# New places in on-chip memory for the operands of an encoder's matmuls

## The chip, the cores and the metric

The kernel runs on one core of a Trainium2 chip. The metric is device time in microseconds (us) of one execution; less is better. The core has five engines: TensorE (PE) multiplies matrices, VectorE (DVE), ScalarE (ACT) and GpSimd (POOL) work element by element, and SyncE (SP) issues most DMA transfers. The on-chip memory holds tiles of 128 partitions; a tile has the same byte place in every partition, and this case is about that place. A matmul on TensorE has two operands in that memory: the stationary one (128 columns), which a weight load (PEld in the profile) brings into the array, and the moving one (here 256 or 512 columns), which streams through it. The sum goes to PSUM, a separate memory.

## The reference

Two encoder layers over 512 tokens of width 1024, 16 heads of 64, all in float32. Cut to what matters:

```python
for layer in range(2):
    h = rms_norm(x, norm_mix_pre[layer])
    h = neighbourhood_attention(h, ...) if layer == 0 else dilated_attention(h, ...)
    x = x + rms_norm(h, norm_mix_post[layer])
    h = rms_norm(x, norm_ffn_pre[layer])
    h = (silu(h @ w_gate[layer]) * (h @ w_up[layer])) @ w_down[layer]     # d_ff = 2816
    x = x + rms_norm(h, norm_ffn_post[layer])
```

Layer 0 attends over an 8 x 64 grid in windows with a learned bias; layer 1 over three dilations (1, 4, 16), which are merged by their softmax denominators. Each mixer begins with products for q, k and v and ends with an output product.

## The kernel before, in words

**Products.** Every float32 operand of a large product is split into a rounded high part and a low remainder, both in the type fp32r (`split`, L365 on ACT and L366 on DVE). One product is then three matmuls (`mm3`, L377 to L379): high by high, high by low, low by high. Blocks of 2 x 2 are multiplied with seven products instead of eight (`Seven`, `Values`, `down`); the sums of operands that this needs are made on POOL and DVE, or by DMA.

**Stages in order of time.** Values of layer 0 (tiles `vp_n`), its q and k units (`pp_n`) with the window attention between them, the output product (`yo`), gate and up products (`gu`, from 258 us to 495 us), the down product (`yd`, to 597 us); then layer 1: values (`vp_d`, `vd`, to 739 us), q and k units (`pp_d`, to 1073 us) with the dilated attention between them, and again `yo`, `gu` (1143 us to 1373 us) and `yd` (to 1477 us). In all stages but two the moving operand has 256 columns; in `yo` and `yd` it has 512.

**Who lies where.** `rxa` and `rxc` hold the transposed activations that are operands; `rxb` holds three more pairs of them for the mixers. The weights, split, lie in eight slots (`h_...`, `l_...` from `wslot`), and one of the seven weight operands alternates between `vmem` and an end of `rxc` (`w22_ring`). `mem` holds hidden activations and what attention needs. `wm`, `memc`, `ao`, `akl` are tiles that follow each other in the same place at the end of memory. In `gu`, `pp_n` and `pp_d` weights are stationary and activations move; in `vp`, `vd`, `yo` and `yd` activations are stationary and weights move. For `yd` the split activations lie in a ring of five places in `rxc`, and the split weights in the eight slots.

**Places.** The tile pools lay tiles out one after the other. Before, the start of each, in bytes modulo 512, is

| tile | before | changed |
|---|---|---|
| `rxa`, `rxc`, `mem` | 160 | 128 |
| `vmem` | 160 | 448 |
| `rxc` from element 80 (`rxs`, new) | | 448 |
| raw weights, slots `h_...` and `l_...` | 480 | 448 |
| `rxb` | 480 | 128 |
| `wm` | 480 | 128 |
| `ao`, `akl`, `memc` | 480 | 480 |

160 and 480 are 32 more than a multiple of 64; 128 and 448 are multiples of 64. Operands are cut from the tiles at multiples of 256 bytes or more.

**Order.** The order of the work on each engine is written by a planner inside the kernel (`Order`): it takes the recorded instructions with their dependences, estimates each one's time (`_cost`), runs eight passes over them, and pins the best order on every engine. It knows sizes and types and nothing of places. Each wait on a chip is a semaphore that another engine raises.

## Time and profile before

| | |
|---|---|
| median of 3 runs | 1484.54 us (1484.52 to 1489.98) |
| the profiled execution | 1487.69 us; its span, first to last instruction, 1485.9 us |
| granted TensorE clock, mean | 0.996 of full speed |
| PE busy | 1442.8 us, 97% of the span, 10788 matmuls |
| PE weight loads | 1333.1 us, 90% |
| DVE, ACT, POOL busy | 1196.8 us (81%), 904.1 us (61%), 542.4 us (37%) |
| moved by DMA | 253.22 MB, 170 GB/s |

A row of groups gives a line of the kernel, the engine, the operation, the tiles (written <- read; for a matmul the moving operand stands first), the shape, the count, busy time and the mean duration of one. The duration of a matmul is that of its passage through the array; matmuls overlap each other, and what a matmul costs in a dense stream is the distance from its start to the start of the next. This document calls that distance the pace. It is read from the timeline, where each row begins with the start in us and the duration.

### The profile page before, as it was taken

The page shows a single profiled execution, that of the slowest core. Times are in us where ns is not written, and L with a number is a line of the kernel's source. Part 1 is how long each engine was busy: PE and PEld are TensorE (multiplying, and loading weights), DVE is VectorE, ACT ScalarE, POOL GpSimd, SP SyncE. Part 2 cuts the span into 40 slices and gives each one's busy share as a digit, 9 for nine tenths or more (in the row PEclk, how much of TensorE's full clock was granted, in tenths as well). Part 3 has the DMA queues.
Part 4 walks back from the last instruction along what each step waited for, and adds up shares of the span by engine and source line. Part 5 has one row for each costly group of instructions (what it writes and reads, how often), then busy time and mean ns, then how long its engine had stood idle before and what let it go on. Part 6 is the DMA issues. An engine that isn't in the chain of part 4 may idle for free.

```text
span 1485.9 us, 27934 instructions
## 1 busy us (share of the span) xinstructions
PE 1442.8 (97%) x10788; PEld 1333.1 (90%) x10788; DVE 1196.8 (81%) x1876; ACT 904.1 (61%) x1819; POOL 542.4 (37%) x398
## 2 busy tenths in 40 slices
PE   7999999899999999999999999999999999999997
PEld 6988877899999888899999999989977999999886
DVE  5499967699889788797689788787657989998877
ACT  4478874555555567544467778876675654555664
POOL 5345425544231001665555444334204644330001
PEclk9999999899999999999999999999999999999999
DMA  5346487677333664435433343333766788834662
GB/s 200 139 177 179 155 286 206 227 221 212 114 112 114 204 220 162 168 126 187 142 100 101 93 145 116 100 133 103 237 206 214 200 243 243 252 126 149 203 208 92
DMA packets 86645, 253.22 MB, mean 170 GB/s; under 512 B 19312, under 2 KB 31600, under 8 KB 84464
## 3 DMA queue, kind: packets, MB, share of 16 engines
q1 hardware_dynamic: 77696, 197.69, 40.4%
q0 software_dynamic: 8672, 53.48, 13.9%
q8 instruction: 85, 1.39, 0.4%
q14 instruction: 48, 0.39, 0.1%
q10 hardware_dynamic: 144, 0.26, 0.0%
HBM read 229.24 MB, written 68.29 MB: 200 GB/s over the span
## 4 chain that ended last, share of the span: by engine, by line
PE 77%; DVE 8%; ACT 7%; DMA 3%; issue 3%; POOL 1%; SPq 0%; POOLq 0%; DVEq 0%; ACTq 0%
PE gu L377 10%; PE gu L378 9%; PE gu L379 9%; PE pp_d L377 5%; PE pp_d L379 4%; PE pp_d L378 4%; PE yd_s L377 3%; PE yd_s L379 3%; PE yd_s L378 3%; PE yd_pp L377 2%; PE yd_pp L379 2%; PE yd_pp L378 2%; PE sb L1274 2%; PE yo L377 2%; PE yo L379 1%
## 5 line engine op out<-in xcount | busy, mean ns | idle before, releaser
L585 POOL TENSOR_TENSOR rs_yd<-v_yd,mhalf 128x1 f32<-128x1 f32 x8 | 8.3, 1043 | 261.3 <-DVE v_yd L583 261.3
L378 PE MATMUL gu<-rxa,h_b 128*128 128x256 f32 x352 | 100.0, 284 | 2.5 <-DVE rxa L602 2.5
L377 PE MATMUL gu<-rxc,h_a 128*128 128x256 f32 x352 | 99.7, 285 | 2.0 <-ACT h_a L365 1.2
L377 PE MATMUL gu<-rxa,h_c 128*128 128x256 f32 x352 | 99.7, 283 | 1.3 <-DVE memc L839 1.1
L378 PE MATMUL gu<-rxc,h_a 128*128 128x256 f32 x352 | 99.7, 284 | 1.2 <-DVE rxc L602 1.0
L377 PE MATMUL gu<-rxa,h_b 128*128 128x256 f32 x352 | 99.7, 284 | 1.2 <-ACT rxa L601 1.2
L379 PE MATMUL gu<-rxa,l_b 128*128 128x256 f32 x352 | 99.6, 283 | 0.2 <-DVE l_b L366 0.2
L379 PE MATMUL gu<-rxc,l_a 128*128 128x256 f32 x352 | 99.1, 282 | 0.0
L378 PE MATMUL gu<-rxa,h_c 128*128 128x256 f32 x352 | 98.7, 280 | 0.0
L379 PE MATMUL gu<-rxa,l_c 128*128 128x256 f32 x352 | 98.3, 280 | 0.0
L365 ACT ACTIVATE rxc<-mem 128x512 fp32r<-128x512 f32 (+2 forms) x90 | 55.9, 624 | 65.9 <-PE yd_pp L378 33.8
L445 POOL TENSOR_TENSOR r_d<-r_d 128x512 f32<-128x512 f32 x24 | 36.1, 1506 | 161.0 <-DVE l_ad L366 122.9
L445 POOL TENSOR_TENSOR r_gu<-r_gu 128x512 f32<-128x512 f32 x20 | 30.6, 1529 | 149.8 <-DVE l_a L366 102.4
L366 DVE TENSOR_TENSOR rxc<-mem,rxc 128x512 fp32r<-128x512 f32 (+2 forms) x90 | 64.4, 719 | 19.5 <-ACT rxc L365 19.2
L445 POOL TENSOR_TENSOR raw<-raw 128x512 f32<-128x512 f32 x24 | 38.0, 1582 | 99.4 <-DVE l_a L366 74.7
L378 PEld LDWEIGHTS gu<-rxa,h_b 128*128 128x128 f32 x352 | 67.6, 192 | 2.7 <-DVE rxa L602 2.7
L377 PEld LDWEIGHTS gu<-rxc,h_a 128*128 128x128 f32 x352 | 67.1, 192 | 2.8 <-ACT h_a L365 1.4
L377 PEld LDWEIGHTS gu<-rxa,h_c 128*128 128x128 f32 x352 | 66.5, 189 | 2.9 <-DVE memc L839 1.3
L378 PEld LDWEIGHTS gu<-rxc,h_a 128*128 128x128 f32 x352 | 67.2, 191 | 1.8 <-DVE rxc L602 1.8
L377 PEld LDWEIGHTS gu<-rxa,h_b 128*128 128x128 f32 x352 | 67.3, 192 | 1.5 <-ACT rxa L601 1.4
L1238 ACT ACTIVATE mem<-mem 128x256 f32<-128x256 f32 x128 | 63.8, 504 | 7.5 <-DVE mem L1237 7.3
L379 PEld LDWEIGHTS gu<-rxa,l_b 128*128 128x128 f32 x352 | 67.4, 191 | 0.4 <-DVE l_b L366 0.4
(610 smaller groups left out, 6157.7 us busy)
## 6 DMA issues: line engine op xcount, KB each, us to landing
wsum<-wd POOLq DMA_DIRECT2D x24, 1408.0 KB, 12.1
r_d<-dil_qk SPq DMA_DIRECT2D x48, 512.0 KB, 4.1
raw<-wg SPq DMA_DIRECT2D x24, 512.0 KB, 5.1
raw<-wu SPq DMA_DIRECT2D x24, 512.0 KB, 8.4
wsum<-wsum POOLq DMA_DIRECT2D x8, 1408.0 KB, 10.3
raw<-wsum SPq DMA_DIRECT2D x22, 512.0 KB, 4.3
r_gu<-wg SPq DMA_DIRECT2D x20, 512.0 KB, 3.8
r_gu<-wu SPq DMA_DIRECT2D x20, 512.0 KB, 4.9
```

Of the source, the lines that this page charges most:

```text
L365: act.activation(h, src, AF.Copy)
L366: dve.tensor_sub(l, src, h.bitcast(F32))
L377: i = pe.matmul(o, s[0], m[0], start=start, stop=False, skip_group_check=True)
L378: pe.matmul(o, s[0], m[1], start=False, stop=False, skip_group_check=True)
L379: pe.matmul(o, s[1], m[0], start=False, stop=stop, skip_group_check=True)
L445: self.added = e[0].tensor_add(q[0], q[0], q[2])
L585: pool.tensor_tensor(r, v, mhalf, op=ALU.pow)
L1238: act.activation(pr[:, f], pr[:, f], AF.Exp, bias=st[:, c:c + 1], scale=-1.0, accum_out=st[:, c + 2:c + 3])
L1274: pe.matmul(ss[hd][:, f0:f0 + P], qf[rw, block(c)], kf[rw, block(c)], start=True, stop=True)
```

## The change

The tiles and parts of tiles move to the places in the right column above. By the roles of the operands: moving activations of the 256-wide products and stationary activations of `vp`, `vd` and `yo` come to 128, split weights to 448. In `yd`, stationary activations come to 448, where its moving weights are. In `yo`, most moving weights come to 128 (`wm`, `rxb`, parts of `rxa`), where its stationary activations are. Counted over the fp32r matmuls of the program, by the distance of the two operands' starts modulo 512:

| moving operand | distance | before | changed |
|---|---|---|---|
| 256 wide | 192 or 320 bytes | 6232 | 7880 |
| 256 wide | same place | 1760 | 48 |
| 256 wide | other | 64 | 128 |
| 512 wide | 192 bytes | 1244 | 112 |
| 512 wide | same place | 64 | 1196 |

Besides, twenty one-column tiles of the norms become columns of one tile `few_small`, and the constant `mhalf` moves behind the weight slots. The tile `wm` gets 88 unused columns.

```diff
-MEM, ARENA = 14544, 9 * D
+MEM, ARENA = 14544, 9 * D + 88
+SHIFT = 80
...
+    zpool = ctx.enter_context(tc.tile_pool(name="zpool", bufs=1))
...
-    mhalf = cpool.tile([P, 1], F32, name="mhalf")
-    dve.memset(mhalf, -0.5)
...
     rxc = cpool.tile([P, 5 * D + 256], F32R, name="rxc")
+
+    mem = cpool.tile([P, MEM], F32, name="mem")
     vmem = cpool.tile([P, D], F32R, name="vmem")
 
-    mem = cpool.tile([P, MEM], F32, name="mem")
+    few_small = cpool.tile([P, 32], F32, name="few_small")
+    mhalf = zpool.tile([P, 48], F32, name="mhalf")[:, 0:1]
+    dve.memset(mhalf, -0.5)
+
+    rxs = rxc[:, SHIFT:SHIFT + 5 * D]
...
-    small_ = cycle(range(20))
+    small_ = cycle([few_small[:, i:i + 1] for i in range(20)])
...
-            return tagged(cpool, [P, n], F32, f"small_o{next(small_)}", name, 1)
+            return next(small_)
...
-        v_ = w22_ring(rxc[:, 4 * D:5 * D])
+        v_ = w22_ring(rxs[:, 4 * D:])
...
-        us = [None] * 2 + [hl(wm, 0, D), (wm[:, 2 * D:], vmem), hl(rxa, 8, D)] + [hl(rxb, 2 * i, D) for i in range(3)]
+        us = [None] * 2 + [hl(wm, 0, D), (wm[:, 2 * D:3 * D], vmem), hl(rxa, 8, D)] + [hl(rxb, 2 * i, D) for i in range(3)]
...
-        hl_ = ring(rxc, 0, D, 5)
+        hl_ = ring(rxs, 0, D, 5)
...
-    with arena("wm0", 3 * D, "right", F32R) as wm:
+    with arena("wm0", 3 * D + 88, "right", F32R) as wm:
...
-    q_, k_, kl_, ost_ = rxc[:, 0:D], rxc[:, D:2 * D], rxc[:, 2 * D:3 * D], ring(rxc, 3 * D, D, 1)
-    w22_ = w22_ring(rxc[:, 4 * D:5 * D])
+    q_, k_, kl_, ost_ = rxc[:, 0:D], rxs[:, D:2 * D], rxs[:, 2 * D:3 * D], ring(rxs, 3 * D, D, 1)
+    w22_ = w22_ring(rxs[:, 4 * D:])
...
-    vus, vslots = {}, cycle([hl(rxc, 0, D), hl(rxc, 2, D), (vmem, rxc[:, 4 * D:5 * D])])
+    vus, vslots = {}, cycle([hl(rxs, 0, D), hl(rxs, 2, D), (vmem, rxs[:, 4 * D:])])
```

The instructions stay the same in number and kind on every engine: 10390 matmuls before they are expanded for the chip, and as many after. Their order stays the same too, but for 46 matmuls, and a few rows of ACT and DVE beside them, at one place: PE at the end of `gu` of layer 0, where its last two units (numbers 20 and 21) meet the first products of `yd`. Before, PE has there:

```order
L379 MATMUL gu_21_5096<-rxa,l_b_21_5341 128x256
L377 MATMUL gu_21_5096<-rxa,h_b_21_5340 128x256
L378 MATMUL gu_21_5096<-rxa,h_b_21_5340 128x256
L379 MATMUL gu_21_5096<-rxa,l_b_21_5341 128x256
L377 MATMUL gu_20_4980<-rxa,h_c_20_5318 128x256
L378 MATMUL gu_20_4980<-rxa,h_c_20_5318 128x256
L379 MATMUL gu_20_4980<-rxa,l_c_20_5319 128x256
L377 MATMUL gu_20_4980<-rxa,h_c_20_5318 128x256
```

and in the changed kernel, at the same place:

```order
L385 MATMUL gu_21_5072<-rxa,l_b_21_5317 128x256
L383 MATMUL gu_21_5072<-rxa,h_b_21_5316 128x256
L383 MATMUL gu_20_4956<-rxa,h_c_20_5294 128x256
L384 MATMUL gu_20_4956<-rxa,h_c_20_5294 128x256
L385 MATMUL gu_20_4956<-rxa,l_c_20_5295 128x256
L383 MATMUL gu_20_4956<-rxa,h_c_20_5294 128x256
L384 MATMUL gu_20_4956<-rxa,h_c_20_5294 128x256
L385 MATMUL gu_20_4956<-rxa,l_c_20_5295 128x256
```

Two of the `gu_21` products with `rxa` moved some rows back, and those of `gu_20` came forward; the operands, the shapes and the number of rows are the same.

On POOL, the norms of the output product raise to the power -0.5 (L585 before, L591 now) between sums of weight operands. Before:

```order
L445 TENSOR_TENSOR r_gu_0_2881<-r_gu_0_2881 128x512
L585 TENSOR_TENSOR rs_yo_0_2594<-v_yo_0_2592,mhalf 128x1
L446 TENSOR_TENSOR r_gu_0_2881<-r_gu_0_2881 128x512
L873 DMA wsum_82<-wd 128x2x1408
L445 TENSOR_TENSOR r_gu_1_2916<-r_gu_1_2916 128x512
L585 TENSOR_TENSOR rs_yo_1_2607<-v_yo_1_2605,mhalf 128x1
```

and now:

```order
L451 TENSOR_TENSOR r_gu_0_2857<-r_gu_0_2857 128x512
L591 TENSOR_TENSOR few_small<-few_small,mhalf 128x1
L452 TENSOR_TENSOR r_gu_0_2857<-r_gu_0_2857 128x512
L879 DMA wsum_86<-wd 128x2x1408
L451 TENSOR_TENSOR r_gu_1_2892<-r_gu_1_2892 128x512
L591 TENSOR_TENSOR few_small<-few_small,mhalf 128x1
```

Nothing moved here; the small tiles have one name in place of many, and all engines together wait on semaphores at three instructions more than before, of some 4500.

More of the change, by code (lines that the diff above doesn't have):

```diff
@@ L1429, in encoder_kernel @@
     inner.close()
-    with arena("wm1", 3 * D, "right", F32R) as wm:
+    with arena("wm1", 3 * D + 88, "right", F32R) as wm:
         mix_out(1, a["dil_o"], rxb, wm, load_block)
```

## Prediction

> **What bounds the kernel now.** I read the page first: busy times, then the chain of work that ended last.
>
> ```profile
> span 1485.9 us, 27934 instructions
> PE 1442.8 (97%) x10788; PEld 1333.1 (90%) x10788; DVE 1196.8 (81%) x1876; ACT 904.1 (61%) x1819; POOL 542.4 (37%) x398
> PE 77%; DVE 8%; ACT 7%; DMA 3%; issue 3%; POOL 1%; SPq 0%; POOLq 0%; DVEq 0%; ACTq 0%
> ```
>
> TensorE is busy for 97% of the span and makes 77% of the chain. So time is gained or lost by what one matmul costs in a dense stream. That is the pace, from one start to the next, and the change touches nothing else on TensorE. I therefore looked in the timeline of PE for stretches without a wait and divided the distance of two rows by the matmuls between them. First, one piece of the values of layer 1, in which nothing waits:
>
> ```profile
> 700.01 0.28 PE L379 MATMUL vd<-rxc,rxb 128*128 128x256 f32 x1
> ...
> 711.91 0.28 PE L377 MATMUL vd<-h_cd,rxb 128*128 128x256 f32 x1
> 711.92 0.19 PEld L378 LDWEIGHTS vd<-l_cd,rxb 128*128 128x128 f32 x1
> 712.03 0.28 PE L378 MATMUL vd<-l_cd,rxb 128*128 128x256 f32 x1
> ...
> 714.79 0.28 PE L377 MATMUL vd<-rxc,rxa 128*128 128x256 f32 x1
> ```
>
> From 700.01 to 711.91 are 105 matmuls: 113.3 ns each. In them the two operands start 320 or 192 bytes apart modulo 512 (`rxc` and `vmem` at 160 against `rxb` at 480, the slots at 480 against `rxa` at 160). From 711.91 to 714.79 are 24: 120.0 ns each. There both lie at 480 (slot `h_cd` or `l_cd`, and `rxb`). The shape and the stage are the same; the places differ. The rows of 711.92 and 712.03 show what can meet: the weight load of the next matmul begins 0.01 us after the start of the present one, so that stationary and moving operand are read at the same time, from 480 both.
>
> Then a piece of `gu` of layer 0, and two of `yd`, of layer 0 and of layer 1:
>
> ```profile
> 443.21 0.28 PE L379 MATMUL gu<-rxa,vmem 128*128 128x256 f32 x1
> ...
> 453.69 0.28 PE L377 MATMUL gu<-rxc,h_a 128*128 128x256 f32 x1
> ...
> 500.04 0.39 PE L379 MATMUL yd_pp<-h_d0p,rxc 128*128 128x512 f32 x1
> ...
> 539.87 0.39 PE L379 MATMUL yd_s<-h_d0s,rxc 128*128 128x512 f32 x1
> ...
> 1380.05 0.40 PE L379 MATMUL yd_pp<-h_d1p,rxc 128*128 128x512 f32 x1
> ...
> 1419.94 0.40 PE L379 MATMUL yd_s<-h_d1s,rxc 128*128 128x512 f32 x1
> ```
>
> `gu`: 89 matmuls in 10.48 us, 117.8 ns, although all but the first of these operands are 320 bytes apart (weights at 480, activations at 160). `yd`: 174 in 39.83 us, 228.9 ns, and in layer 1 171 in 39.89 us, 233.3 ns, with the same operands at the same places. So place is not all: a stream finds one of two paces when it starts after a wait, and keeps it.
>
> The numbers have a common step. 120.0 less 113.3 is 6.7 ns, and 113.3 is 17 such steps, 120.0 is 18, 233.3 is 35. Sixteen steps for 256 columns would be 16 columns, or 64 bytes, a step. An operand of 1024 bytes that starts 32 bytes beyond a multiple of 64, as all of them do before, touches 17 pieces of 64 bytes and not 16. That fits a best pace of 17 steps, though it doesn't prove it: a fixed cost of one step fits as well.
>
> What could stop a faster TensorE? DVE, which makes the operands. The windows of both gate and up stages:
>
> ```profile
> core 0: us, PE busy (x) PEld busy (x) DVE busy (x) ACT busy (x) POOL busy (x), PEclk, DMA share, GB/s
> 258.00:488.00 230.00, 224.51 (x1860) 222.97 (x1861) 200.94 (x256) 123.41 (x211) 82.07 (x54) 0.98 0.54 170
> 1143.00:1366.00 223.00, 220.85 (x1858) 219.01 (x1857) 200.69 (x256) 121.88 (x211) 89.34 (x61) 1.00 0.72 211
> 495.00:587.00 92.00, 92.00 (x404) 75.50 (x403) 79.48 (x107) 62.34 (x94) 3.40 (x3) 1.00 0.61 196
> ```
>
> In `gu` DVE is busy for 401.6 of 453 us, 89%; in `yd` for 79.5 of 92.0, 86%, and PE without a break.
>
> **The change part by part.** It removes and adds no instruction on any engine; 46 matmuls of 10390 change rank at one place, which I cost at nothing, since they stand in the same `gu` stream with the same operands. One column of `few_small` in place of a small tile costs nothing either: three more waits in some 4600, at the norms of `yo`, whose work stands beside products. If that cover went, each would cost about one such operation on POOL, 1.04 us by the page, 3 us in all:
>
> ```profile
> L585 POOL TENSOR_TENSOR rs_yd<-v_yd,mhalf 128x1 f32<-128x1 f32 x8 | 8.3, 1043 | 261.3 <-DVE v_yd L583 261.3
> ```
>
> What is left is the pace. It has two causes: the distance of the operands, and the start at a multiple of 64. The second is in no row of before, since no large operand starts at one there. Bounds for a 256-wide matmul, then: above, 117.8 ns, the slower pace that a distance of 320 has now; nothing in the trace says that distance alone forbids it. Below, the weight load: each matmul needs one of 128 columns.
>
> ```profile
> 851.32 1.03 PE L1334 MATMUL t<-ident,mem 128*128 128x128 f32 x8
> L1334 PE MATMUL t<-ident,mem 128*128 128x128 f32 x256 | 36.6, 276 | 0.0
> ```
>
> Eight transposes of 128 columns, each with a weight load, take 1.03 us from the first start to the last end; less one duration of 0.276, over seven distances, that is 108 ns. So a 256-wide matmul lies between 108 and 117.8 ns. I take 112: between 108 and the 113.3 that the trace already has, nearer to the row. For a 512-wide matmul the same piece counting gives 33 steps with the present start and 32 without: 220 to 233.3 ns; I take 227, a little under the better pace of now, since what it loses beyond 33 steps is not explained.
>
> *Gate and up.* 22 units of 84 matmuls in each layer, 3696 in all. 528 of them lie at the same place now (`vmem` and the end of `rxc` against `rxa`), yet the piece from 443.21 shows 117.8 for the mixture, and some stretches run at 113.3; I take 117.6 as their mean. 117.6 less 112 is 5.6 ns, times 3696: 20.7 us. DVE would then be busy for 401.6 of 432 us, 93%, and what TensorE gains it waits for now and then: I let two thirds through, 14 us. Without DVE in the way it would be 20.7; if DVE lets nothing through, 0.
>
> *The other 256-wide products.* 8056 in the program less 3696 are 4360. Of these 1232 lie at the same place now (1760 less 528), at 120.0; the rest I put midway between 113.3 and 117.8, at 115.6. Mean 116.8; to 112 it is 4.8 ns, times 4360: 21 us. In these stages attention stands between the products, and the chain gives 23% to others than PE; again two thirds, 14 us.
>
> *The 512-wide products.* 1308, at 228.9 and 233.3 in about equal parts, 231 in the mean; to 227 it is 4 ns, 5 us. PE has no break there, so all of it counts.
>
> Sum: 14 + 14 + 5 = 33 us off a span of 1485.9, 1453 us. The profiled execution took 1487.69 us, 1.8 more than its span, and 3.2 more than the median of the runs, 1484.54. Off the median it makes 1451.5, so 1452 us.
>
> A rule speaks against all of this. The Trainium skill, SBUF — State Buffer, section Specifications (TRN2), gives lines of 16 bytes, by which a start at 32 beyond a multiple of 64 is as good as one at 0. The Trainium skill, TensorE: Matmul & The Clock Gate, section Step-by-step: what each phase is for, says that loading the next weights takes no read bandwidth from the running matmul, by which the distance of the operands should not matter. The trace disagrees with the second: 120.0 against 113.3 ns in neighbouring rows. On the first no row of before decides. By both the time would stay at 1484, which is the rival of no change below. The same page's section Back-to-back issue gap gives columns over 2.4 GHz plus 2.5 ns, an estimate of 109.2 ns for 256 columns; it would lie inside my bounds, and with it the two 256-wide terms would be some 31 and 33 us before what DVE holds back.
>
> **The rivals.**
>
> *All of the pace is gained.* The 256-wide matmuls come to 108 ns and the 512-wide ones to 220. Terms: 9.6 x 3696 = 35 us, 8.8 x 4360 = 38 us, 11 x 1308 = 14 us; with two thirds of the first two, 63 us: 1422. Half way to it from my case, 1437. For it: the exact 17 steps. Against: DVE at 200.7 of 223 us. Chance 0.22 that the time is under 1440.
>
> *DVE becomes the bound.* Pace falls as I say, but `gu` gains nothing, as DVE's two-operand work there waits for POOL and ACT as it does now; then 14 + 5 = 19 us: 1466, and with less elsewhere 1476. For it: 89% busy. Against: the waits of PE for DVE in the windows of `gu` are few now (224.5 and 220.9 us busy of 230 and 223). Chance 0.12.
>
> *No change: the start at 64 bytes does nothing.* What stays is the distance: 1712 matmuls fewer at the same place, at 120.0 less 117.8, 4 us, of which two thirds: 1482; if these came to 113.3, 11 us, two thirds of it 8: 1477. For it: `gu` at 117.8 with a distance of 320, and the two paces of `yd` at the same places. Chance 0.14.
>
> *Slower: the same place in the 512-wide products.* They go the other way: from 64 at the same place to 1196. In the 256-wide rows the same place costs one step of 6.7 ns; a moving operand twice as long could meet the weight load twice, 13.3 ns. 1132 more by 13.3 are 15 us, all on the path as PE has no break in `yd`; if the 64 bytes gain nothing and only the 4 us of distance come back, 1496. It decides from about 10 ns a matmul on, beyond what the other terms bring if they fail. Against it stand the few that lie at the same place now (`vmem` against `rxa` in `yo`; columns: shortest, median and longest duration) beside others of that line that don't:
>
> ```profile
> L378 PE MATMUL yo<-wm,rxa x16: 388/392/505, 218.2 to 1132.8; 128*128 128x512 f32 x16
> L378 PE MATMUL yo<-vmem,rxa x16: 388/393/401, 219.5 to 1134.2; 128*128 128x512 f32 x16
> ```
>
> 392 and 393 ns: no step between them. Chance 0.07.
>
> **How the numbers follow.** My case, 1440 to 1466, has 0.45; the full gain 0.22; DVE as the bound 0.12; no change 0.14; slower 0.07. A measurement of this kernel tells about 0.5% from no change, 7.4 us: faster is below 1477.1, slower above 1492. The first three cases and a little of the fourth's lower end make 0.80 for faster; the rest of the fourth 0.13 for the same; 0.07 for slower. The range goes from 1425, where the full gain with two thirds ends, to 1484, where no change begins to be a loss; what lies outside are the slower case and the ends of the others.
>
> **What would show it.** In the changed trace the neighbouring pieces of `vd` must have one pace, 113.3 or less, with no 120.0 left; this is the surest step. The pace of `gu` must be under 117.8 in long pieces; if there are rows under 113, the start at 64 bytes is what does it. `yd` must be at 229 or less in both layers; 240 would be the slower rival. In `gu`, PE's share of busy time must fall and waits on DVE rise by some 7 us. Wrong would be the prediction if `gu` keeps 117.8, or if paces fall and the span doesn't.

## The result: 0.75% faster, about a third of the forecast gain

The changed kernel takes 1477.45 us (median), the kernel before, on the same chip, 1489.98 us. The ratio is 0.9925, with a 95% interval of 0.9908 to 0.9943: 11 us faster by the ratio (12.5 by the medians), where 32 were forecast. The profiled execution of the changed kernel took 1475.85 us with a span of 1474.0, 11.9 us less than the span of before; this is the difference that the rest explains. On the page of the changed kernel the busy times and the chain now read:

```profile
span 1474.0 us, 27934 instructions
PE 1425.7 (97%) x10788; PEld 1317.0 (89%) x10788; DVE 1200.5 (81%) x1876; ACT 902.7 (61%) x1819; POOL 541.4 (37%) x398
PE 66%; DVE 15%; ACT 8%; DMA 4%; issue 4%; POOL 1%; SPq 0%; POOLq 0%; DVEq 0%; ACTq 0%
```

PE is busy for 17.1 us less and its weight loads (PEld) for 16.1; DVE, ACT and POOL stay within 4 us of before. PE's share of the chain falls from 77% to 66% and DVE's rises from 8% to 15%: part of what the products gained has turned into waits, as the table below shows.

The paces come from the timeline of PE, as in the prediction: first and last row of a stretch without a break, divided by the matmuls between them in the program. (`mm3` stands six lines lower in the changed kernel, at L383 to L385.) Values of layer 0, values of layer 1, gate and up of layer 1, and the down product of layer 1:

```profile
36.60 0.28 PE L383 MATMUL vp_n<-h_n,rxa 128*128 128x256 f32 x1
...
60.74 0.29 PE L383 MATMUL pp_n<-rxa,h_an 128*128 128x256 f32 x1
...
694.70 0.28 PE L384 MATMUL vd<-rxc,rxb 128*128 128x256 f32 x1
...
717.94 0.33 PE L383 MATMUL vd<-rxc,rxb 128*128 128x256 f32 x1
...
1262.75 0.28 PE L384 MATMUL gu<-rxa,h_c 128*128 128x256 f32 x1
...
1316.35 0.28 PE L385 MATMUL gu<-rxa,l_b 128*128 128x256 f32 x1
...
1364.62 0.39 PE L384 MATMUL yd_pp<-l_d1p,rxc 128*128 128x512 f32 x1
...
1451.88 0.39 PE L385 MATMUL yd_s<-h_d1x2b,rxc 128*128 128x512 f32 x1
```

`vp_n`: 205 matmuls at 117.8 ns, as before. `vd`: 205 at 113.4. `gu`: 473 in a row at 113.3 ns, where before the long stretches ran at 117.8. `yd` of layer 1: 385 at 226.7 ns, where it was 233.3. The 120.0 of before is in no stretch of the changed kernel. Nor is anything with 256 columns below 113.3.

The next table sets every start on PE of both profiled executions against the program. A distance from one start to the next of up to 124 ns (245 for 512 columns) counts as pace. Of a longer one, 116 ns (237) counts as pace and the rest as stall. "Net" is the difference of the two sums; pace in ns, the rest in us, before -> after.

```
stage           matmuls   pace             at that pace     stalls         net
gu, layer 0       1848    117.44 -> 113.97   217.0 -> 210.6   10.7 -> 12.0   -5.0
gu, layer 1       1848    117.40 -> 114.28   217.0 -> 211.2    5.3 ->  7.4   -3.7
vp_n               384    117.62 -> 117.62    45.2 ->  45.2    2.6 ->  2.6    0.0
pp_n               672    116.97 -> 115.72    78.6 ->  77.8    9.6 -> 11.6   +1.1
vp_d               192    117.68 -> 117.06    22.6 ->  22.5    4.4 ->  5.4   +0.8
vd                 840    116.02 -> 115.05    97.5 ->  96.6    4.5 ->  4.0   -1.3
pp_d              2016    116.62 -> 115.36   235.1 -> 232.6   16.2 -> 18.7    0.0
yo, both layers    384    230.9  -> 230.2     88.7 ->  88.4    4.1 ->  4.3    0.0
yd, layer 0        462    229.06 -> 226.89   105.8 -> 104.8    0.1 ->  0.1   -1.0
yd, layer 1        461    233.24 -> 226.76   107.5 -> 104.5    0.0 ->  0.0   -3.0
all others                                                                   +0.3
```

The rows add up to -11.8 us. At the pace alone they give 20.8 us, and the stalls grow by 8.6. Gate and up give 8.7 us net and the down product 4.0; everything else together loses 0.9. All of this is from one execution of each kernel.

The windows of the two `gu` stages (columns as in the prediction: length, then busy time of each engine) show how full DVE is there:

```profile
259.20:491.20 232.00, 225.24 (x1905) 222.15 (x1906) 206.39 (x263) 125.91 (x216) 83.68 (x54) 0.99 0.55 173
1137.60:1364.50 226.90, 223.88 (x1908) 220.39 (x1908) 207.37 (x264) 124.82 (x216) 88.98 (x61) 1.00 0.71 212
```

DVE is busy for 413.8 of 458.9 us, 90%; PE's idle time is 6.8 and 3.0 us. PE's waits for DVE in `gu`, added up, are 6.4 us, before 5.1; in the products of queries and keys, `pp_n` and `pp_d`, they are 7.5, before 4.2. Two rows that show the latter, in the view of PE's waits (total us, times, longest), of before:

```profile
PE pp_d L377 <- DVE pp_d L435: 1.2, 2, 0.8
...
PE pp_n L377 <- DVE mem L686: 0.5, 1, 0.5
```

and of the changed kernel:

```profile
PE pp_n L383 <- DVE mem L692: 2.0, 1, 2.0
...
PE pp_d L383 <- DVE pp_d L441: 1.6, 4, 0.9
```

### The profile page after: what moved, and what is told of

Read it like the earlier page. It is cut to its first block, busy times and chain, and to the rows that moved or that the text cites. A ratio compares the mean times of both kernels' runs of the same rounds, so it can differ in the third digit from the quotient of the medians.

```text
span 1474.0 us, 27934 instructions
## 1 busy us (share of the span) xinstructions
PE 1425.7 (97%) x10788; PEld 1317.0 (89%) x10788; DVE 1200.5 (81%) x1876; ACT 902.7 (61%) x1819; POOL 541.4 (37%) x398
## 4 chain that ended last, share of the span: by engine, by line
PE 66%; DVE 15%; ACT 8%; DMA 4%; issue 4%; POOL 1%; SPq 0%; POOLq 0%; DVEq 0%; ACTq 0%
PE gu L383 7%; PE gu L384 7%; PE gu L385 7%; PE pp_d L383 4%; PE pp_d L385 4%; PE pp_d L384 3%; PE yd_s L385 3%; PE yd_s L384 3%; PE yd_s L383 3%; PE yd_pp L384 2%; PE yd_pp L385 2%; PE yd_pp L383 2%; PE yo L383 2%; PE yo L385 1%; PE yo L384 1%
## 5 line engine op out<-in xcount | busy, mean ns | idle before, releaser
L591 POOL TENSOR_TENSOR rs_yd<-v_yd,mhalf 128x1 f32<-128x1 f32 x8 | 9.5, 1184 | 255.2 <-DVE v_yd L589 255.2
L383 PE MATMUL gu<-rxa,h_c 128*128 128x256 f32 x352 | 99.3, 282 | 3.1 <-DVE memc L845 1.4
L383 PE MATMUL gu<-rxc,h_a 128*128 128x256 f32 x352 | 97.7, 279 | 2.4 <-ACT h_a L371 1.5
L383 PE MATMUL gu<-rxa,h_b 128*128 128x256 f32 x352 | 98.6, 281 | 1.2 <-ACT rxa L607 1.2
L384 PE MATMUL gu<-rxc,h_a 128*128 128x256 f32 x352 | 98.0, 279 | 1.1 <-DVE rxc L608 1.0
L385 PE MATMUL gu<-rxa,l_b 128*128 128x256 f32 x352 | 98.6, 280 | 0.3 <-DVE l_b L372 0.3
L385 PE MATMUL gu<-rxc,l_a 128*128 128x256 f32 x352 | 97.3, 277 | 0.0
L385 PE MATMUL gu<-rxa,l_c 128*128 128x256 f32 x352 | 97.1, 277 | 0.0
L451 POOL TENSOR_TENSOR r_d<-r_d 128x512 f32<-128x512 f32 x24 | 33.4, 1391 | 162.2 <-DVE l_ad L372 123.5
L372 DVE TENSOR_TENSOR rxc<-mem,rxc 128x512 fp32r<-128x512 f32 (+2 forms) x90 | 64.3, 717 | 17.3 <-ACT rxc L371 17.1
L383 PEld LDWEIGHTS gu<-rxa,h_c 128*128 128x128 f32 x352 | 66.1, 188 | 5.9 <-DVE memc L847 2.0
L383 PEld LDWEIGHTS gu<-rxc,h_a 128*128 128x128 f32 x352 | 65.9, 188 | 3.4 <-ACT h_a L371 2.1
L383 PEld LDWEIGHTS gu<-rxa,h_b 128*128 128x128 f32 x352 | 67.0, 191 | 1.6 <-ACT rxa L607 1.4
L385 PEld LDWEIGHTS gu<-rxa,l_b 128*128 128x128 f32 x352 | 67.3, 191 | 0.5 <-DVE l_b L372 0.5
## 6 DMA issues: line engine op xcount, KB each, us to landing
wsum<-wd POOLq DMA_DIRECT2D x24, 1408.0 KB, 11.9
```

Source lines behind the costliest of these rows:

```text
L372: dve.tensor_sub(l, src, h.bitcast(F32))
L383: i = pe.matmul(o, s[0], m[0], start=start, stop=False, skip_group_check=True)
L384: pe.matmul(o, s[0], m[1], start=False, stop=False, skip_group_check=True)
L385: pe.matmul(o, s[1], m[0], start=False, stop=stop, skip_group_check=True)
L451: self.added = e[0].tensor_add(q[0], q[0], q[2])
L591: pool.tensor_tensor(r, v, mhalf, op=ALU.pow)
```

## The experiments

From here on, **distance** is the start of the moving operand less that of the stationary one, modulo 512 bytes. `gu` has its weights stationary (448 after the change) and its activations moving (128): a distance of 192, and it was 192 before as well, from 480 to 160. The value products `vp_n`, `vp_d` and `vd` have the activations stationary and the weights moving: 320. `yd` goes from 320 to 0.

**The start alone.** The kernel before, with every large operand 32 bytes nearer to the front: all start at a multiple of 64, and every distance is what it was.

```
-MEM, ARENA = 14544, 9 * D
+MEM, ARENA = 14544, 9 * D + 8
...
+    zpool = ctx.enter_context(tc.tile_pool(name="zpool", bufs=1))
...
-    mhalf = cpool.tile([P, 1], F32, name="mhalf")
-    dve.memset(mhalf, -0.5)
...
+    few_small = cpool.tile([P, 32], F32, name="few_small")
+    mhalf = zpool.tile([P, 128], F32, name="mhalf")[:, 0:1]
+    dve.memset(mhalf, -0.5)
...
```

> Only the start at a multiple of 64 bytes: all tiles move by 32 bytes, the distances of the operands stay those of before (1712 of the 256-wide matmuls at the same place, the 512-wide ones 192 apart). If the start is what quickens the stream, gate and up go from 117.4 to about 114 ns a matmul and the time to 0.993 to 0.995 of before. If the distance does it, gate and up stay at 117 ns, with pieces at 120, the down product at 229 to 233, and the ratio is 1.000 within 0.002.

Measured: 1487.92 us against 1487.36; ratio 1.000, 0.9988 to 1.0013. In the timeline of PE the same two paces stand side by side as before:

```profile
659.01 0.28 PE L379 MATMUL vd<-rxc,rxb 128*128 128x256 f32 x1
...
670.80 0.28 PE L379 MATMUL vd<-h_cd,rxb 128*128 128x256 f32 x1
...
673.68 0.28 PE L379 MATMUL vd<-rxc,rxa 128*128 128x256 f32 x1
```

104 matmuls at 113.4 ns, then 24 at 120.0, with 448 in place of 480 and 128 in place of 160. `gu` has 117.5 and 117.3, `yd` 229.0 and 233.3. A start at a multiple of 64 does nothing, and with that the larger of the two causes on which the forecast rested is gone.

**The distance alone.** The changed kernel, with every large operand 32 bytes further: the distances of the change, with the starts of before.

```
-MEM, ARENA = 14544, 9 * D + 88
+MEM, ARENA = 14544, 9 * D + 80
...
+    on = cpool.tile([P, 8], F32, name="on")
+    dve.memset(on, 0.0)
```

> Only the distances: the changed kernel with every tile 32 bytes further, so that no large operand starts at a multiple of 64. If the distance does it (pieces at the same place throw the stream into the slower phase, and these are gone), gate and up run at 114 ns, the down product at 227, and the ratio to before is 0.9925 as for the change. If the start does it, gate and up stay at 117 and only the loss of the 120 ns pieces shows: 0.997 to 0.999.

Measured: 1478.79 us; ratio 0.9943, 0.9929 to 0.9958, which overlaps the interval of the change. So the distance gives the gain. The timeline holds two stretches of `gu`, of layer 0 and of layer 1:

```profile
312.08 0.28 PE L386 MATMUL gu<-rxa,rxc 128*128 128x256 f32 x1
...
364.67 0.28 PE L385 MATMUL gu<-rxa,h_b 128*128 128x256 f32 x1
...
1250.45 0.28 PE L386 MATMUL gu<-rxc,h_a 128*128 128x256 f32 x1
...
1334.66 0.32 PE L385 MATMUL gu<-rxa,vmem 128*128 128x256 f32 x1
```

464 matmuls at 113.3 ns, and 715 at 117.8, with every operand at the same distance of 192. The same distance allows both paces, and a stream keeps for hundreds of matmuls the one that it found; which of the two it has is called its **phase** here. `gu` came to 114.4 in layer 0 and 116.9 in layer 1.

**The down product apart again.** The changed kernel, with the hidden values of `yd` back at 128 against 448 (distance 320).

```
     def ffn(layer, stack, memc):
-        hl_ = ring(rxs, 0, D, 5)
+        hl_ = ring(rxc, 0, D, 5)
```

> The changed kernel with the ring of split activations of the down product back at 128, 192 bytes from its weights at 448. If the same place is what brings the down product from 229 and 233 ns to 227, it goes back to 229 to 233, and the time is 1 to 6 us over the change: ratio to before 0.994 to 0.996. If it was the start at 64, 227 ns stay and the ratio is 0.9925.

Measured: 1479.57 us; ratio 0.9954, 0.9936 to 0.9972. `yd` of layer 1, where the change has 226.7:

```profile
1364.53 0.40 PE L385 MATMUL yd_pp<-h_d1p,rxc 128*128 128x512 f32 x1
...
1468.13 0.39 PE L385 MATMUL yd_s<-h_d1x2b,rxc 128*128 128x512 f32 x1
```

444 matmuls at 233.3 ns, and 229.1 in the mean of layer 0: the numbers of before. Against the paces of the change this is 1.0 us in layer 0 and 3.0 in layer 1. The intervals of the two times overlap, so it is the pace that shows the step: the same place makes the whole gain of `yd`.

**A piece of `gu` at the same place again.** The changed kernel, with those weights of `gu` that lie in `vmem` and in the last part of `rxc` at 128, where the activations start, so that 528 of its 3696 matmuls have a distance of 0, as before. (`vmem` serves `pp_n`, `pp_d` and `vd` too: 272 of their matmuls come to a distance of 0 with it.)

```
+    vmem = cpool.tile([P, D], F32R, name="vmem")
     mem = cpool.tile([P, MEM], F32, name="mem")
-    vmem = cpool.tile([P, D], F32R, name="vmem")
...
-        v_ = w22_ring(rxs[:, 4 * D:])
+        v_ = w22_ring(rxc[:, 4 * D:5 * D])
```

> The changed kernel with one of the seven weight operands (vmem, and in gate and up the end of rxc) back at the place of the activations, 128: some 800 of the 256-wide matmuls at the same place again. If pieces at the same place cost 120 ns and leave a slower stream behind them, gate and up go from 114 back to about 117 ns and the time is some 8 us over the change: ratio to before 0.997 to 0.999. If such a piece costs only itself, 528 matmuls by 6.7 ns, 3.5 us: 0.9945 to 0.995, and the matmuls after a piece run at 113.3.

Measured: 1483.08 us; ratio 0.9973, 0.9962 to 0.9984. `gu` is back at 117.5 in both layers. The timeline shows how, at the start of a stretch of 971 matmuls without a break; the rows whose second operand, the weights, is `rxc` or `vmem` are those at the same place:

```profile
312.09 0.28 PE L383 MATMUL gu<-rxa,h_c 128*128 128x256 f32 x1
...
313.45 0.28 PE L383 MATMUL gu<-rxa,rxc 128*128 128x256 f32 x1
...
314.17 0.28 PE L383 MATMUL gu<-rxc,h_a 128*128 128x256 f32 x1
...
323.12 0.28 PE L383 MATMUL gu<-rxa,vmem 128*128 128x256 f32 x1
...
324.56 0.28 PE L384 MATMUL gu<-rxc,h_a 128*128 128x256 f32 x1
...
333.27 0.28 PE L383 MATMUL gu<-rxa,rxc 128*128 128x256 f32 x1
```

12 matmuls at 113.3 ns, 6 at 120.0 at the same place, and then 76 at 117.8; 12 at 120.0, 74 at 117.8, and so to the end. The operands of the 12, the 76 and the 74 have the same distance. The short piece costs little itself: 528 at 120 rather than 114 ns are 3 us. What it leaves behind is the larger part: 3168 others at 117 rather than 114 ns, some 10 us. Together that is the gain of the change in `gu`, at the pace.

**The grid of paces.** A kernel of streams alone: one group of matmuls after the other, 128 stationary columns, moving 256 or 512 wide, at every distance in steps of 32 bytes, with the stationary operand at 0 or 32.

```
+    for n, t in ((256, 14), (512, 8)):
+        for lead in (0, 64, 192):
+            for a in (0, 32):
+                for d in range(0, 512, 32):
+                    stream(a, d, n, t=t, lead=lead)
```

> Nothing of the encoder is computed: the output is left out, and only streams of matmuls run, each after a wait, on constant data. 256 and 512 columns; stationary operand at 0 or 32 modulo 64; the moving one at every distance from 0 to 480 in steps of 32; each with three leads (none, one matmul of 64 columns, one of 192) that change how the stream begins; some distances off by 4, 16 or 48 bytes; stationary operands of 32 and 64 columns. If the pace hangs on the distance alone: 120 ns at 0, 113.3 or 117.8 elsewhere, whatever the start. If the start at 64 counts: lower for operands that both start at a multiple of 64, 108 to 110 ns. If the seventeenth step is the weight load, it goes away with 32 stationary columns (106.7 to 109 ns); if it is of the moving operand, 113.3 stays. A piece at the same place within a stream: if phases last, the rest of that stream runs at 117.8, else at 113.3. At 512: 227 ns at the same place, 229 to 233 elsewhere.

In the timeline equal rows are put together: start, length of all, and their number. The pace is the length less one duration (0.28 us, or 0.39), over the number less one. With the stationary operand at 32, distances 0, 64 and 192 with 256 columns; with it at 0, the same three with 512:

```profile
130.77 3.40 PE L34 MATMUL b<-w 128*128 128x256 f32 x27
...
142.33 2.87 PE L34 MATMUL b<-w 128*128 128x256 f32 x23
...
164.29 2.88 PE L34 MATMUL b<-w 128*128 128x256 f32 x24
...
578.25 3.11 PE L34 MATMUL b<-w 128*128 128x512 f32 x13
...
590.83 2.68 PE L34 MATMUL b<-w 128*128 128x512 f32 x11
...
614.81 3.20 PE L34 MATMUL b<-w 128*128 128x512 f32 x13
```

120.0, 117.7 and 113.0 ns (113.3 by the single starts); 226.7, 229.0 and 234 ns. The whole grid, as the mean of the later half of each stream (where a cell has two numbers, streams at the same places had one or the other, by what stood ahead of them). The first two streams, with 148 and 133 ns, are left out; the granted clock of the first 50 us was 0.87:

```
distance            0      32     64     96     128          160          192          224
256 columns         120.0  116.7  117.8  120.0  118.7        117.3-118.7  113.3/117.8  118.3
512 columns         226.7  233.3  228.9  233.3  232-233.8    234.0-234.5  233.3-233.7  233.4
distance            256    288    320    352    384          416          448          480
256 columns         120.0  116.7  117.8  120.0  118.7-120.0  117.3-120.0  113.3/117.8  118.4
512 columns         226.7  233.3  228.9  233.3  232-233.8    234.5        233.3-233.7  233.4
```

The second half repeats the first: what counts is the distance modulo 256 bytes, not 512. Without a matmul ahead of the stream, the rows for a stationary operand at 0 and at 32 agree, as in the run with the start alone; behind one of 192 columns, the distance of 192 had 113.3 with the one and 117.8 with the other. For 256 columns the best distance is 192, for 512 it is 0. So with the distance of 64 that `vp_n` has on this scale, starting from rest, the pace is 117.8, which is what it shows before and after.

**All large operands 256 apart.** The changed kernel with the weights at 384 and the activations at 128. Modulo 512 most 256-wide products then have their operands 256 apart; modulo 256 all have them at one place.

```
-MEM, ARENA = 14544, 9 * D + 88
+MEM, ARENA = 14544, 9 * D + 24
...
-SHIFT = 80
+SHIFT = 64
...
+    mhalf = cpool.tile([P, 112], F32, name="mhalf")[:, 0:1]
```

> The changed kernel with the weights at 384 in place of 448, and rxb and wm at 384: every pair of operands is then 256 bytes apart or at the same place. If the memory repeats every 512 bytes, as the change supposes, 256 is a distance like others: 113 to 118 ns a matmul and a ratio to before of 0.99 to 1.00. If it repeats every 256, as the streams alone showed (120.0 ns at 0 and at 256, 113.3 at 192 and 448), every 256-wide matmul takes 120 ns: some 5 ns by 7900 over the change, 40 us at most, less where others wait: ratio 1.005 to 1.02. The down product then keeps 227 ns.

Measured: 1497.5 us; ratio 1.0058, 1.0039 to 1.0078. A stretch of `gu`:

```profile
314.56 0.28 PE L384 MATMUL gu<-rxa,rxc 128*128 128x256 f32 x1
...
457.36 0.29 PE L382 MATMUL gu<-rxa,rxc 128*128 128x256 f32 x1
```

1190 matmuls in a row at 120.0 ns; `yd` keeps 227.0. Two operands 256 bytes apart behave as if they lay at one place. The kernel is slower than before, in which most distances were 64 or 192 on this scale.

**Less work for DVE.** Did DVE eat the gain? Two kernels, the one before and the changed one, each without two sums on DVE in each unit of gate and up (the weights then hold other values; all transfers and products stay). The planner gives them another order on PE than the full kernels have, at some 2000 of the 10788 places, but nearly the same to both: 200 places differ between the two.

```
-            e[2].tensor_add(q[3], q[0], q[3])
+            if e[2] is not dve:
+                e[2].tensor_add(q[3], q[0], q[3])
...
-            self.adds[3].tensor_add(self.q[1], self.q[3], self.q[1])
+            if self.adds[3] is not dve:
+                self.adds[3].tensor_add(self.q[1], self.q[3], self.q[1])
```

> The kernel before with the two sums of weight operands that DVE makes for each gate and up unit left out, so that its products there are of other operands. DVE has some 1.9 us less to do in each of 44 units. If DVE holds TensorE back there before the change already, the time falls by 5 us or more; if TensorE's pace alone sets these stages, it stays within 3 us of before.

> The changed kernel with the same two sums of each unit left out. If DVE ate part of the gain in gate and up, the distance between this and its partner without the change is larger than between the full kernels: 15 us or more in place of 11. If the pace of TensorE is all there is, the distance stays at 9 to 13 us.

Busy times on the page of the first:

```profile
PE 1442.0 (97%) x10788; PEld 1334.0 (90%) x10788; DVE 1134.7 (76%) x1788; ACT 902.7 (61%) x1819; POOL 538.5 (36%) x398
```

and of the second:

```profile
PE 1426.7 (97%) x10788; PEld 1320.0 (90%) x10788; DVE 1136.4 (77%) x1788; ACT 903.6 (61%) x1819; POOL 539.3 (37%) x398
```

Of DVE's work 62 and 64 us are gone. Measured against the kernel before: 1484.68 us, 0.9973 (0.9962 to 0.9984), and 1474.87 us, 0.9916 (0.9896 to 0.9937). Their quotient is 0.9943, and by their intervals taken together it is known to about 0.0024; 0.9925, what the change gives with all of DVE's work, lies inside. With less work for DVE the change brings no more than with it. `gu` comes to 114.5 and 114.6 ns in the second, no better than 114.0 and 114.3, and the change takes 8.6 us off `gu` between the two light kernels, 8.7 between the full ones. So DVE, with that much work, holds neither the pace of `gu` nor what the change brings there.

**What a stream remembers.** Streams alone again: 36 matmuls at a distance of 192 (weights W at 448 stationary, activations A at 128 moving), then 12 at one place, then 72 at 192 again, and variants of it; after that, moving operands of other widths.

```
+    A, W = 128, 448
+    for lead in (0, 64):
+        chain([(W, A, 12), (A, A, 4), (W, A, 24)], lead)
...
+        chain([(W, A, 12), (A, W, 24)], lead)
+        chain([(A, W, 12), (W, A, 24)], lead)
+        chain([(W, A, 12), (W, W, 4), (W, A, 24)], lead)
+        chain([(W, A, 12), (A, W, 24), (W, A, 24)], lead)
```

> Nothing of the encoder is computed: only streams of matmuls on constant data. Widths of 128 to 512 columns, with 32 and with 128 stationary columns. If the seventeenth step is a fixed cost of a matmul, the pace is the width by 0.417 ns plus 6.7 ns at each width; if it is a rate, the width by 0.443 ns: 85 ns at 192, 113.3 at 256, 170 at 384, 226.7 at 512. Chains: stationary at 448 and moving at 128, then four triples with both at 128, then again 448 and 128: if a piece at the same place leaves the slower phase behind it, the rest runs at 117.8 after having begun at 113.3, else 113.3. Stationary at 128 and moving at 448 after 448 and 128: 117.8 if the pace hangs on the pair alone, 113.3 if the phase carries over. Leads of 32 to 224 columns: the same pair starts at 113.3 with some and at 117.8 with others. 512 columns with leads: 228.9 with some and 233.3 with others where the distance is 320, always 226.7 at the same place.

The first chain is the three rows from 209.76; the third chain of the excerpt (A stationary and W moving, then W and A) the two from 257.54. The two from 368.24 are the first and the last piece of the fourth chain, and the two from 386.23 the second and the third piece of the fifth, both behind a matmul of 64 columns. The rows ahead of all these are widths of 128, 320 and 384 columns:

```profile
123.97 3.40 PE L34 MATMUL b<-w 128*128 128x128 f32 x29
...
151.61 4.56 PE L34 MATMUL b<-w 128*128 128x320 f32 x30
...
163.23 5.55 PE L34 MATMUL b<-w 128*128 128x384 f32 x31
...
209.76 3.45 PE L34 MATMUL b<-w 128*128 128x256 f32 x29
...
213.39 1.48 PE L34 MATMUL b<-w 128*128 128x256 f32 x11
...
214.94 8.40 PE L34 MATMUL b<-w 128*128 128x256 f32 x70
...
257.54 3.23 PE L34 MATMUL b<-w 128*128 128x256 f32 x26
...
261.31 8.29 PE L34 MATMUL b<-w 128*128 128x256 f32 x69
...
368.24 3.23 PE L34 MATMUL b<-w 128*128 128x256 f32 x26
...
373.34 7.87 PE L34 MATMUL b<-w 128*128 128x256 f32 x68
...
386.23 7.98 PE L34 MATMUL b<-w 128*128 128x256 f32 x69
...
394.75 7.94 PE L34 MATMUL b<-w 128*128 128x256 f32 x66
```

113.2 ns, then 120.0 at one place, then 117.7 for all that follows, with the operands of the first 36: the same as in `gu` with its piece at one place. If in the middle piece the moving operand goes to W instead of the stationary one to A, the stream is at 113.3 afterwards, even where it began at 118.0 (the rows of 368.24 and 373.34). So the piece at one place sets the phase, to either side. A stream that begins at 320 runs at 118.0, and stays at 117.8 when it goes on to 192. One that begins at 192 with 113.3 keeps it when it goes on to 320, but is at 117.8 when it then returns to 192 (386.23 and 394.75; so it was with and without a matmul ahead). This would explain why `vd` has stretches of 113.4 at a distance at which `vp_n` hardly ever has: its stream may enter that distance at the fast pace. In 512 columns no such memory was seen: 228.9 at 320, 233.3 at 192 and 226.7 to 227.0 at one place, whatever stood ahead.

The widths bear on the step of 6.7 ns. 128 and 192 columns take 111.6 ns each with 128 stationary columns, and 192 take 87 to 88 with 32 stationary ones, so that 128 stationary columns set a floor of 111.6. 320 columns take 146.7 ns, 22 steps where 20 pieces of 16 columns would make 20; 384 take 173.3, 26 where it would be 24; 256 take 17 at the best and 512 take 34. That isn't a fixed step for each matmul, nor one for the start of the operand. One step for each 256 columns begun fits these four, but not the 448 columns of the same kernel: 202.5 ns, where 30 steps would be 200.0. The widths other than 256 and 512 were run at the distances 0 and 192 alone.

**The value products at a better distance.** If only the distance counts, moving the weights of the value products by 128 bytes (distance 192 on the scale of 256) must bring them to 113.3. This needed the slots as one tile with 32 more columns, and put another matmul at over 4400 of the 10788 places in PE's order.

```
+    slots = spool.tile([P, 8 * D + 32], F32R, name="slots")
...
+    rxv = rxc[:, 48:48 + 5 * D]
...
-        u = units2(srcs, name, raw=raw)
+        u = units2(srcs, name, raw=raw, on=32)
...
-    vus, vslots = {}, cycle([hl(rxs, 0, D), hl(rxs, 2, D), (vmem, rxs[:, 4 * D:])])
+    vus, vslots = {}, cycle([hl(rxv, 0, D), hl(rxv, 2, D), (vmem_[:, 32:], rxv[:, 4 * D:])])
```

> The changed kernel with the weights of the value products (vp, vd) 128 bytes further on, so that there too the moving operand starts 192 bytes beyond the stationary one modulo 256, as in gate and up; rxb and wm at 384. If the pace hangs on that distance and on the phase in which a stream starts, vp and vd go from 115 to 117.5 ns towards 113.3: 1416 matmuls by up to 4 ns, 2 to 5 us under the change, ratio to before 0.989 to 0.992. If the direction doesn't matter, as the table of distances before the chip said (192 or 320 alike), nothing: 0.9925.

`vp_n`, which ran at 117.8 in nearly all its stretches at the old distance:

```profile
36.35 0.28 PE L392 MATMUL vp_n<-slots,rxa 128*128 128x256 f32 x1
...
62.64 0.28 PE L392 MATMUL vp_n<-slots,rxa 128*128 128x256 f32 x1
```

232 matmuls at 113.3 ns; `vp_d` falls from 117.1 to 114.7, while `vd` has 115.0. In `vp_n` and `vp_d` the pace comes as the distance says. The time doesn't: 1492.24 us, ratio 1.0017, 1.0002 to 1.0033. With the new order the matmuls outside the large products (all others, in the table's terms) take 9.5 us more than before and `pp_n` 6.0, `gu` of layer 1 has 16.2 us of stalls, and `pp_d` takes 5.5 less. The order moves more than the pace does, so this says nothing of what the distance alone would bring in the value products.

**The change again, and three of seven.** The changed kernel once more, as a measure of how far it varies; and, with the order kept, the changed kernel with three of the seven weights of `vd` moved by 128 bytes.

```
+    rxv = rxc[:, 48:48 + 5 * D]
...
-    vus, vslots = {}, cycle([hl(rxs, 0, D), hl(rxs, 2, D), (vmem, rxs[:, 4 * D:])])
+    vus, vslots = {}, cycle([hl(rxv, 0, D), hl(rxv, 2, D), (vmem_[:, 32:], rxv[:, 4 * D:])])
```

> The change itself, unaltered, beside the version with the value weights moved: ratio to before 0.991 to 0.994. In gate and up each stage is at 113 to 114 ns if it starts in the quick phase and at up to 117 ns if not, by chance of the start.

> The changed kernel with three of the seven weight operands of the value units of layer 1 (those in rxc and vmem) 128 bytes further on or back, so that 360 matmuls of vd have their moving operand 192 bytes beyond the stationary one modulo 256, as in gate and up; the order on the engines stays that of the change. If that distance lets a stream into the quick phase, and the phase carries over to the 480 matmuls that stay at 320, vd goes from 115.1 to 117.5 ns a matmul (both were seen with the change) to 113.5 to 115: 1 to 3 us, ratio to before 0.990 to 0.993. If the direction doesn't matter, vd stays at 117.5 in this run or the next: ratio 0.9925.

The change: 1477.8 us, 0.9923 (0.9905 to 0.9941), the same ratio; but `gu` has 115.1 and 114.8 in its profile and `vd` 117.5, where the first execution had 114.0, 114.3 and 115.1. Which phase a stream finds is thus not the same in every execution. `vd` is at 117.5 or 117.6 with the distance alone, with the down product apart and in the light kernel with the change too, so that its 115.1 in the first execution is the exception. Three of seven: 1475.74 us, 0.9916 (0.9892 to 0.9941), with `vd` at 116.6. That isn't told apart from the change. A kernel with all value weights moved and the old order was not run.

## Why the prediction was right in direction and wrong in size

**What bounds the kernel** was right: the instructions are the same, and all that is gained, 12.7 us, comes from the pace in `gu` and `yd`, of which the rest takes 0.9 back. That **"a stream finds one of two paces when it starts after a wait, and keeps it"** was right as to the two paces, and is the key to the result; it stands in the prediction as an observation, but no term of the sum was built on it. A wait isn't needed, though: a piece of 6 matmuls at another place turned 113.3 into 117.8 in mid-stream.

**The step that failed is "I take 112", for every 256-wide matmul alike.** The number rested on the start at a multiple of 64, which "is in no row of before", and on counting 17 pieces of 64 bytes. The start alone gave a ratio of 1.000. The grid gave the same set of paces for 0 and 32. The other explanation that the prediction named, a fixed cost of one step, is wrong as well, since 512 columns pay it twice (34 steps at the best, where 32 would be without it). The bound below, 108 ns, was too low besides: it came from transposes, and with 128 stationary columns these streams never went under 111.6. Nothing with 256 columns went under 113.3, so the 113.3 that the trace already had was the end, not a step on the way. The estimate of 109.2 ns by the Trainium skill, TensorE: Matmul & The Clock Gate, section Back-to-back issue gap, isn't reached either: 113.3 is the least measured here.

The number itself is the smaller part of the miss. With 113.3 in place of 112 the two 256-wide terms would be 15.9 and 15.3 us at the pace, and with the same two thirds the sum 26 us in place of 33, where 11 to 12 were measured. The larger part is that it was put on all of them alike: a stream finds 113.3 in some places and phases only, so that gate and up came to 114.1 in the mean and the other products to 115.7; and in the stages of these others, of which two thirds were let through, nothing of the pace came out.

Term by term, at the pace and net:

- *Gate and up*, forecast 20.7 at the pace and 14 net: 12.2 and 8.7. The mean went from 117.4 to 114.1 and not to 112. Why it moved is not the reason given: the distance of the stream is 192 before and after. What the change did was to take out the 528 matmuls at one place, which put the stream into the slower phase each time; with them back, `gu` is at 117.5. "Two thirds through" was close (8.7 of 12.2), though not as a limit of DVE: with 64 us less of its work the change gains no more.
- *The other 256-wide products*, forecast 21 at the pace and 14 net: 4.3 and nothing (a loss of 0.6). This is the largest miss. The 1232 matmuls at 120.0 did get a better distance, but the value products have 64 on the scale of 256 and the pace of 117.8 there, unless a stream brings 113.3 along. The change even took a good distance away: 240 matmuls of `vd` (`rxc` or `vmem` against `rxb`) lay at 192 before, at 114.2 to 114.6 ns, and lie at 64 on that scale now, at 117.7 to 117.9 when the change was run again. So the 1.3 us that the table gives to `vd` are luck of that execution: its 840 matmuls, stalls with them, took 101.9 us before, 100.7 in it, and 103.5 the second time. What `pp_n` and `pp_d` gained, 3.3 us, came back as stalls, 4.5 us. That attention and the making of weights set the time in these stages fits this, but no run shows it apart.
- *The 512-wide products*, forecast 5: 4.3 at the pace, 4.0 net. The pace was forecast as 227 and is 226.8. The reason given was again the start, and it is the distance: with the hidden values apart, 233.3 and 229.1 return.

**The rivals.** *No change: the start does nothing* had the mechanism right. Its price for the distance, some 3 to 8 us net, is short of the 11 us, because it counted the matmuls at one place and not those after them. That the 1477 at its lower end is what was measured is luck: the kernel before took 1489.98 us beside the change, and the prediction counted from 1484.54. *DVE becomes the bound* falls with the two lighter kernels. *All of the pace is gained* falls with the 113.3. *Slower through the same place in the 512-wide products* is wrong by sign: the same place costs 256 columns one step, and is the best for 512. The few rows of `yo` that spoke against it, 392 and 393 ns, were right not to show a loss, though they are durations and not paces, and so couldn't show a gain.

**What would show it.** No 120.0 is left in the changed kernel, as said. "One pace" in `vd` is not: it holds both 113.4 and 117.8. `gu` under 117.8 in long pieces is right, `yd` at 229 or less in both layers is right, and rows under 113 there are none. PE's share of busy time in `gu` fell as said, but little: from 97.6 and 99.0% to 97.1 and 98.7% in the windows shown. Waits on DVE in `gu` rose by 1.3 us, not by 7.

By the Trainium skill, TensorE: Matmul & The Clock Gate, section Step-by-step: what each phase is for, loading the next weights takes no read bandwidth from the running matmul. By that the distance of the two operands should not matter, and it does: 113.3 to 120.0 ns for the same work in the grid. But the load isn't shown to be the cause: with 32 stationary columns, a quarter of the load, 256 moving columns still take 113.4 to 117.7 ns, though at one place they take 117.7 and 113.4 and not 120.0.

**What stays open.** Before, and with the hidden values apart, `yd` runs at 229.1 in layer 0 and at 233.2 in layer 1, with the same places in both. In the lighter kernel before, layer 1 has 229.0. The streams alone never had 233.3 at that distance. What picks the phase at the start of a stream is open too: in the second kernel of streams, at a distance of 192, 64 columns ahead of it gave either pace, 32 and 96 gave 117.8, and 128 to 224 gave 113.3; in the grid 192 columns ahead gave either. Why a return from 320 to 192 ends the fast phase is open as well. And nothing here shows which part of the memory or of PE has the period of 256 bytes.

## What to carry to other kernels

When a dense stream shows two paces, look at what stands ahead of the slow one as well as at its own operands: here a seventh of the matmuls, at a bad place, slowed the other six sevenths. Count what a move of operands takes away as well as what it gives: 240 matmuls of `vd` lost their good distance. Judge the start and the distance of operands apart, each by a kernel that moves only the one; a hypothesis of alignment that fits the number of steps is cheap to form, and one run took it away. A shorter pace is worth its matmuls only in a stage where PE has no break (`yd`: all of it; `gu`: 7 parts in 10; the products beside attention: nothing).

## What the runs showed of the hardware

- For two operands of 4 bytes per element and 128 stationary columns, the pace depends on the distance of their starts modulo 256 bytes: 113.3 to 120.0 ns with 256 moving columns, 226.7 to 234.5 with 512. The best is a distance of 192 for the first and 0 for the second, and 0 is the worst for the first.
- PE's stream has a memory: at a distance of 192 it stays at 113.3 or at 117.8 for hundreds of matmuls (473 and 715 in a row), and 6 matmuls at one place, reached by the stationary operand, are enough to move it from the fast to the slow one. 12 at one place, reached by the moving operand, moved a slow stream to the fast one.
- Starts at a multiple of 64 and of 32 are alike (ratio 1.000). Starts off a multiple of 32 by 16 bytes gave 117.5 to 120.3 ns in the grid, where the others have 113.3 to 120.0; off by 4 bytes, 119.9 to 123.5.
- 128 stationary columns set a floor of 111.6 ns. 256 and 512 moving columns take 17 and 34 steps of 6.67 ns at the best of all distances; 320, 384 and 448 take 22, 26 and 30.4 at the distances of 0 and 192.
